# Where the weight differences of a Strassen-like down projection are made, and in which steps the work beside the second up phase is taken

## The chip, the cores and the metric

One core of a Trainium2 chip runs one program. The metric is the device time in microseconds (us) of one execution; the kernel before was run three times. PE is the matmul engine (PEld its weight loads), DVE the vector engine, ACT the scalar engine, POOL the GpSimd engine, SP the engine that issues most DMAs.

## What is computed

A residual block over 2048 positions of width 1024: a mixer (RG-LRU heads beside gMLP groups) and a gated feed-forward network, each between two RMS norms with scale, shift and gate from a conditioning vector.

```
h  = rmsnorm(x, g_mix_pre) * (1 + sc_m) + sh_m
z  = h @ w_in
y  = concat(rmsnorm(lru(z)), rmsnorm(gmlp(z))) @ w_out
x  = x + gt_m * rmsnorm(y, g_mix_post)
h  = rmsnorm(x, g_ffn_pre) * (1 + sc_f) + sh_f
up = causal_depthwise_conv(h @ w_up)        # 2 * 3072 columns, width 3
g_ff, v_ff = split(up)
y  = (gelu(g_ff) * v_ff) @ w_down           # 3072 -> 1024
x  = x + gt_f * rmsnorm(y, g_ffn_post)
```

Everything is float32. A product of two float32 operands is made of three matmuls: each operand is split into a high half (a cast on ACT) and a low half (source less high half, on DVE), and high*high, high*low and low*high are summed in PSUM.

## The kernel before

The positions are cut into 4 chunks of 512 for the mixer and 2 halves of 1024 for the feed-forward network. The program is one long list that is written out in Python; a planner then orders it by priority (the place in the list, less an offset where `high_priority` says so) with a model of the engines, lays the tiles into pools with a fixed number of slots, and adds the waits. Each engine, and each engine's DMA queue, runs its own list in order. Work that runs beside the main list is written as generators in a list `bg`; `tick()` takes one step of each, `drain()` takes all that are left on the spot.

**The mixer** (lines 830 to 854) takes chunk after chunk: `mixer_z(c)` makes z and its recurrences, `mixer_out(c - 1)` multiplies the chunk before by `w_out`. Beside them run the norms, the conditioning vectors (`ada_task`), and from c = 2 on `w_sums` (line 629). For each of 12 pairs of 128 rows of `w_down` it loads both rows whole (two DMAs of 512 KB on SP's queue), makes four differences of the two rows' halves (four POOL instructions of 128x512) and stores them (two DMAs of 512 KB on POOL's queue) in the DRAM tensor `wsd`. It waits for nothing, so that the planner may place it where POOL is idle, ahead of c = 2 too.

**The up phases** `up_phase(C, f0)` (line 1072), one for each half C of the positions, take 24 blocks f (from f = 2 on in the first) of the gated up projection as seven products instead of eight (`up_pair`, line 1041). Each block ends with a `tick()`. The weights' differences are made in the first and read back in the second. In the second, `first_finals` (line 1254) is started at f = 3: it makes the gate of the feed-forward network (`ada_task(5, 1)`, 21 steps) and then the last norm, gate and residual of the first half of the positions (`final`, line 1087, twice; 12 steps with those around it): 33 steps in all. `drain()` in line 1304 takes what is left after the phase.

**The down phases** `down_fast(C)` (line 1113) have seven products, in the order 11, s1/t1, s2/t2, s4/22, s3/t3, 12/21, 22/t4 (activation part / weight part). A product has 6 sets q, each of 24 matmuls (128x128 by 128x512). `operands` (line 1136) brings a set: an activation part (512 KB) and a weight part (512 KB) are loaded and split. For the four products whose weight part is a t, the weight part is read from `wsd`. Banks A and B of PSUM, four each, hold the sums. Beside the first down phase runs `h2_next`, which makes the activation parts of the second up phase.

Pools that matter: `tp` (36 slots, tag `t4`), `wp` (8, tag `w`: split halves), `rw` (4, tag `wraw`: raw weights), `lp` (3, tag `ld`), `rp` (6, tag `r`). A slot of `rw` is taken by `weight` (line 145) from the load until the low half is made.

Of the kernel before, what the change touches and what calls it, by code (L numbers as in the profile page):

```python
# [10 lines left out]
F32 = mybir.dt.float32  # L11
F32R = mybir.dt.float32r
AF = mybir.ActivationFunctionType
ALU = mybir.AluOpType

P = 128
# [7 lines left out]
NF = 24  # L24
# [16 lines left out]
def block_kernel(ctx: ExitStack, tc: tile.TileContext, xt, cols, rows, wada, wada_r, win_k, win_s, win_v, wgate, wsp, wout, wup, wdown, out):  # L41
# [3 lines left out]
    wp = ctx.enter_context(tc.tile_pool(name="wp", bufs=8))  # L45
    rw = ctx.enter_context(tc.tile_pool(name="rw", bufs=4))
# [7 lines left out]
    vec, act, pool, pe, sync = nc.vector, nc.scalar, nc.gpsimd, nc.tensor, nc.sync  # L54

    def t4(name):
        return tp.tile([P, 2, 512], F32, tag="t4", name=name)
# [25 lines left out]
    def tick():  # L83
        for g in list(bg):
            try:
                next(g)
            except StopIteration:
                bg.remove(g)

    def drain(*gens):  # L90
        for g in gens or list(bg):
            for _ in g:
                pass
            if g in bg:
                bg.remove(g)

    def start(*gens):
        bg.extend(gens)
        return gens
# [13 lines left out]
    def colr(name, j, n):  # L113
        o = _OFF[name] + j
        return prm[:, o:o + n]
# [17 lines left out]
    wsd = dram.tile([NF // 2, 2, P, ND, P], F32, name="wsd")  # L133


    def split(hi, lo, src, eng, leng=None):
        if eng == "act":
            act.copy(out=hi, in_=src)  # L138
        elif eng == "pool":
            pool.tensor_scalar(out=hi, in0=src, scalar1=1.0, scalar2=0.0, op0=ALU.mult, op1=ALU.add)  # L140
        else:
            vec.tensor_copy(out=hi, in_=src)
        (leng or vec).tensor_tensor(out=lo, in0=src, in1=hi.bitcast(F32), op=ALU.subtract)  # L143

    def weight(src, shape, name, eng="act", leng=None, mk=None, ahead=200, mkraw=None):
        with tc.high_priority(offset=ahead):
            raw = mkraw(f"{name}_r") if mkraw else rw.tile(shape, F32, tag="wraw", name=f"{name}_r")
            sync.dma_start(out=raw, in_=src)
            if mk is None:
                hi = wp.tile(shape, F32R, tag="w", name=f"{name}_h")  # L150
                lo = wp.tile(shape, F32R, tag="w", name=f"{name}_l")
            else:
                hi, lo = mk(shape, f"{name}_h"), mk(shape, f"{name}_l")
            split(hi, lo, raw, eng, leng)
        return hi, lo
# [79 lines left out]
    h = {}  # L235

    def x_rms(c, late=2):
        q = SumSq(f"n{c}")
        for j in range(4):
            q.add(load_x(xt, c, j, f"xq{c}"))  # L240
            yield
        yield
        hl = q.done()
        yield from wait(late)
        rx[c] = rms_bcast(hl, 1.0, f"n{c}", "rr", 4)
# [275 lines left out]
    def norm_scale(c, late=2):  # L521

        qs = []
        for tiles, name in zip(HU[c], (f"rl{c}", f"rg{c}")):
            qs.append(SumSq(name))
            for t in tiles:
                qs[-1].add(t)
            yield
        hls = [q.done() for q in qs]
        yield from wait(late)  # L530
        rs = [rms_bcast(hl, 2.0, f"r{n}{c}") for n, hl in zip("lg", hls)]
        yield
        for tiles, gname, r in zip(HU[c], ("g_lru_out", "g_gmlp_out"), rs):
            for j in range(2):
                for b in range(2):
                    t = tiles[j][:, b]
                    vec.scalar_tensor_tensor(out=t, in0=t, scalar=col(gname, 2 * j + b), in1=r, op0=ALU.mult, op1=ALU.mult)
                yield

    def norm_split(c):  # L540
        Y[c] = []
        mk = y4 if c == NC - 1 else h4
        for tiles, name in zip(HU[c], (f"rl{c}", f"rg{c}")):
            for j in range(2):
                yt = mk(f"{name}h{j}"), mk(f"{name}l{j}")
                split(yt[0], yt[1], tiles[j], "act")
                Y[c].append(yt)
                yield

    def mixer_norm(c, late=2):  # L550
        yield from norm_scale(c, late)
        yield from norm_split(c)
# [69 lines left out]
    def h_task(c, rms=True):  # L622
        if rms:
            yield from x_rms(c)
            yield
        h[c] = ([], [])
        yield from build_h(xt, c, h[c], sm, shm, f"x{c}")

    def w_sums():


        for p in range(NF // 2):
            e, o = [rw.tile([P, 8, P], F32, tag="wraw", name=f"ws{p}_{i}") for i in range(2)]
            sync.dma_start(out=e, in_=wdown[2 * p])
            sync.dma_start(out=o, in_=wdown[2 * p + 1])
            yield
            pool.tensor_tensor(out=e[:, :4], in0=e[:, 4:], in1=e[:, :4], op=ALU.subtract)
            pool.tensor_tensor(out=e[:, 4:], in0=o[:, 4:], in1=e[:, 4:], op=ALU.subtract)
            pool.tensor_tensor(out=o[:, 4:], in0=o[:, 4:], in1=e[:, :4], op=ALU.subtract)
            pool.tensor_tensor(out=o[:, :4], in0=o[:, :4], in1=o[:, 4:], op=ALU.subtract)  # L640
            pool.dma_start(out=wsd[p, 0], in_=e)
            pool.dma_start(out=wsd[p, 1], in_=o)
            yield


    wk, adat, acc0, adap = {}, {}, {}, {}

# [175 lines left out]
    for j in range(2):  # L823
        a = t4(f"xc0_{j}")
# [11 lines left out]
    for c in range(1, NC):  # L836
        nt = start(mixer_norm(0, 4) if c == 1 else norm_split(c - 1))
        xr = start(x_rms(c + 1, 8)) if c + 1 < NC else ()
        mixer_z(c)
        drain(*xr, *nt)  # L840
        if c == 1:
            m3, = start(ada_task(3, 1))
        if c == 2:
            m4, = start(ada_task(4, 1))
            wst = start(w_sums())
        if c + 1 < NC:
            ht = start(h_task(c + 1, False), norm_scale(c, 3))
            O, q = mixer_out(c - 1)
            drain(*ht)
            if c == 1:  # L850
                drain(m2)
                vec.tensor_tensor(out=gm, in0=modc[:, 16:24], in1=colr("g_mix_post", 0, 8), op=ALU.mult)
            start(mixer_post(c - 1, O, q))
# [218 lines left out]
    def up_phase(C, f0, on=lambda f: None):  # L1072
        before = None
        for f in range(f0, NF):
            on(f)
            g = up_pair(C, f)
            next(g)
            if before:
                drain(before)
            next(g)  # L1080
            before = g
            tick()
        drain(before)

    od = dram.tile([2, P, ND, 512], F32, name="od")
# [27 lines left out]
    def down_fast(C):  # L1113
# [13 lines left out]
        def w_src(k, q):  # L1127
            if k[0] == "t":
                i, h = {"t1": (0, 0), "t3": (0, 1), "t4": (1, 0), "t2": (1, 1)}[k]
                w = wsd[2 * q:2 * q + 2, i]  # L1130
            else:
                i, h = {"11": (0, 0), "21": (1, 0), "22": (1, 1)}[k]
                w = wdown[4 * q:4 * q + 4].rearrange("(a b) p d c -> a b p d c", b=2)[:, i]
            return w.rearrange("a p d c -> p a d c")[:, :, 4 * h:4 * h + 4]

        def operands(op, k, q):
            with tc.high_priority(offset=150):
                n = f"{op}_{q}"
                n = f"{C}{op}_{q}"
                first = op == "11" and q < 2  # L1140
                raw = t4(f"dgr{n}") if first or C == 0 else lp.tile([P, 2, 512], F32, tag="ld", name=f"dgr{n}")
                sync.dma_start(out=raw, in_=a_src(op, q))
                if C == 0:
                    g = [wp.tile([P, 2, 512], F32R, tag="w", name=f"dg{x}{n}") for x in "hl"]
                else:
                    g = h4(f"dgh{n}"), h4(f"dgl{n}")
                split(g[0], g[1], raw, "act")
                mkraw = (lambda m: tp.tile([P, 2, 4, P], F32, tag="t4", name=m)) if first else None
                w = weight(w_src(k, q), [P, 2, 4, P], f"dw{n}", ahead=0, mkraw=mkraw)
            return g, w  # L1150

        def mm(pt, g, w, a, d, first, stop):
# [91 lines left out]
        hl = rms_split(acc[1], "fr11")  # L1244
# [9 lines left out]
    def first_finals():  # L1254

        yield from ada_task(5, 1)
        vec.tensor_tensor(out=gf, in0=modc[:, 40:48], in1=colr("g_ffn_post", 0, 8), op=ALU.mult)
        for t in range(2):
            hl = rms_split(fsum[0][:, t], f"fr0{t}")
            yield  # L1260
            yield from final(0, t, [None] * 4, hl)
# [22 lines left out]
    O, q = mixer_out(NC - 2, True)  # L1284
# [15 lines left out]
    start(h2_next())  # L1300
    down_fast(0)
    drain()
    up_phase(1, 0, lambda f: start(first_finals()) if f == 3 else None)
    drain()
    down_fast(1)
    drain()
# [70 lines left out]
```

## Time and profile before

| | us |
|---|---|
| median of 3 runs | 2218.62 |
| lowest, highest | 2216.43, 2220.9 |
| the profiled execution | 2214.45 |
| its span, first to last instruction | 2212.4 |

| stage, read from the trace | from us | to us |
|---|---|---|
| mixer | 0 | 718 |
| first up phase | 718 | 1213 |
| first down phase | 1219 | 1450 |
| second up phase | 1450 | 1910 |
| second down phase and end | 1932 | 2212 |

The profile covers one execution. Its page gives the busy time of each engine; the views of the trace beside it give the busy time in chosen stretches, with the number of instructions, the granted clock of PE (1.00 is 2.4 GHz, 0.50 is 1.2 GHz) and the DMA engines' busy share; the groups of instructions by line; who waited for whom; the chain that ended last; and the instructions in order of time. Busy time of PE is modelled, so what a stretch has lost is better read from the number of its matmuls.

### The profile page before, as it was taken

Reading aid. Unit: us, or ns where it says so; the run is one execution under the profiler, and the core shown is the slowest. Engines: PE = TensorE matmul, PEld = TensorE weight load, DVE = VectorE, ACT = ScalarE, POOL = GpSimd, SP = SyncE. Lnnn points to the kernel's source line nnn. Section 1 sums busy time; section 2 is a strip of 40 time slices with the busy share of each in tenths; the row PEclk is TensorE's granted clock in tenths of the full one; section 3 lists DMA queues with packets and bytes.
Section 4 is the critical chain, followed back from the end, with each engine's and each line's share of the span. In section 5 each row is a group of like instructions: output and inputs, shape, how many; then the busy total and the mean of one; then the engine's idle time right before and its main releaser. Section 6 shows DMA issues by size and latency. Waiting matters only on the chain.

```text
span 2212.4 us, 24016 instructions
## 1 busy us (share of the span) xinstructions
PE 2013.4 (91%) x8744; PEld 1647.6 (74%) x8744; DVE 1565.4 (71%) x1703; ACT 950.1 (43%) x1224; POOL 525.1 (24%) x322
## 2 busy tenths in 40 slices
PE   5898948899999899999999999999999999669995
PEld 3686837777787788777877788888888888558884
DVE  7688698698385689998898766655555554754547
ACT  3472632433553555454554555443233333324432
POOL 4454264864320234434432000020000000000000
PEclk8998978998999999999999999999999999779998
DMA  8687578988766578979878656647777776686545
GB/s 316 200 307 279 181 256 309 336 313 309 271 253 242 183 272 330 338 282 360 325 288 316 240 202 217 228 157 256 272 254 264 256 269 241 218 301 212 179 164 152
DMA packets 192678, 572.46 MB, mean 259 GB/s; under 512 B 17456, under 2 KB 17584, under 8 KB 192560
## 3 DMA queue, kind: packets, MB, share of 16 engines
q1 hardware_dynamic: 180496, 527.93, 66.9%
q0 software_dynamic: 10912, 38.80, 4.7%
q10 hardware_dynamic: 1152, 4.19, 0.5%
q8 instruction: 69, 1.13, 0.2%
q14 instruction: 49, 0.40, 0.1%
HBM read 372.67 MB, written 199.23 MB: 259 GB/s over the span
## 4 chain that ended last, share of the span: by engine, by line
PE 59%; DVE 20%; DMA 7%; issue 6%; ACT 5%; POOL 2%; SPq 0%; DVEq 0%; ACTq 0%; POOLq 0%
PE dA L1155 10%; PE dB L1155 9%; PE upa L997 6%; PE upa L998 5%; PE upa L999 5%; PE upc L997 3%; PE upc L998 3%; PE upc L999 3%; DVE a L946 2%; PE upb L999 1%; PE upb L998 1%; DVE acc L665 1%; PE upb L997 1%; DVE x L256 1%; DMA xr<-in_xt_dram 1%
## 5 line engine op out<-in xcount | busy, mean ns | idle before, releaser
L946 DVE SCALAR_TENSOR_TENSOR a<-Rg,prm,a 128x1023 f32<-128x1023 f32 x92 | 127.1, 1382 | 99.3 <-ACT a L944 99.2
L1106 POOL DMA_DIRECT2D out_dram<-do x2 | 2.5, 1252 | 732.4 <-DVE do L1104 732.3
L977 POOL TENSOR_TENSOR wug<-wuv,wug 128x512 f32<-128x512 f32 x24 | 46.9, 1953 | 480.4 <-DVE w L143 480.4
L946 DVE SCALAR_TENSOR_TENSOR a<-Rv,prm,a 128x1023 f32<-128x1023 f32 x92 | 139.3, 1514 | 19.8 <-ACT a L944 19.4
L944 ACT ACTIVATE a<-Rv,prm 128x1024 f32<-128x1024 f32 x46 | 57.2, 1244 | 178.2 <-DVE Rv L1064 178.1
L1155 PE MATMUL dA<-dgh,dw_h 128*128 128x512 f32 x192 | 72.1, 411 | 37.6 <-ACT dw_h L138 19.5
L138 ACT CAST wt<-wug 128x512 fp32r<-128x512 f32 x72 | 44.7, 620 | 115.0 <-POOL wug L981 51.3
L143 DVE TENSOR_TENSOR wt<-wug,wt 128x512 fp32r<-128x512 f32 x72 | 67.9, 943 | 31.0 <-ACT wt L138 30.8
L1002 ACT ACTIVATE a<-a 128x1024 f32<-128x1024 f32 x48 | 50.9, 1060 | 75.9 <-DVE a L946 40.8
L1155 PEld LDWEIGHTS dA<-dgh,dw_h 128*128 128x128 f32 x192 | 38.0, 199 | 47.4 <-ACT dw_h L138 20.9
L143 DVE TENSOR_TENSOR dgl<-dgr,dgh 128x1024 fp32r<-128x1024 f32 x36 | 43.9, 1221 | 41.2 <-ACT dgh L138 41.2
L1155 PE MATMUL dA<-dgh,dw_l 128*128 128x512 f32 x192 | 70.7, 402 | 2.4 <-DVE dw_l L143 2.4
L1155 PE MATMUL dA<-dgl,dw_h 128*128 128x512 f32 x192 | 72.3, 405 | 0.0
L280 DVE SCALAR_TENSOR_TENSOR ada_m<-wada,cact,ada_m 128x1024 f32<-128x1024 f32 x28 | 50.1, 1789 | 27.6 <-DMA wada<-in_wada_r_dram 27.6
L138 ACT CAST dgh<-dgr 128x1024 fp32r<-128x1024 f32 x36 | 37.8, 1049 | 70.0 <-DMA dgr<-gd 30.0
L143 DVE TENSOR_TENSOR dw_l<-dw_r,dw_h 128x1024 fp32r<-128x1024 f32 x36 | 43.8, 1220 | 25.4 <-ACT dw_h L138 25.3
L1005 DVE TENSOR_TENSOR gg<-a,a 128x1024 f32<-128x1024 f32 x48 | 58.3, 1215 | 2.7 <-ACT a L1002 2.6
L944 ACT ACTIVATE a<-Rg,prm 128x1024 f32<-128x1024 f32 x46 | 57.1, 1242 | 1.3
L138 ACT CAST dw_h<-dw_r 128x1024 fp32r<-128x1024 f32 x36 | 37.5, 1047 | 45.1 <-DMA dw_r<-in_wdown_dram 16.2
L143 DVE TENSOR_TENSOR dw1s_l<-dw1s_r,dw1s_h 128x1024 fp32r<-128x1024 f32 x24 | 29.3, 1222 | 38.3 <-ACT dw1s_h L138 34.1
L222 POOL TENSOR_TENSOR rp_s<-rp_s,rp_s 128x1024 f32<-128x1024 f32 x12 | 30.0, 2499 | 91.0 <-ACT rp_s L218 90.9
L1068 ACT COPY Rg<-upa 128x512 f32<-128x512 f32 x46 | 26.8, 583 | 55.0 <-PE upa L999 55.0
(655 smaller groups left out, 6963.3 us busy)
## 6 DMA issues: line engine op xcount, KB each, us to landing
wkd<-wt SPq DMA_DIRECT2D x88, 512.0 KB, 3.8
wkd<-w SPq DMA_DIRECT2D x66, 512.0 KB, 4.6
w<-wkd SPq DMA_DIRECT2D x66, 512.0 KB, 4.1
gd<-gg SPq DMA_DIRECT2D x48, 512.0 KB, 4.4
gsd<-gg SPq DMA_DIRECT2D x48, 512.0 KB, 3.8
wrt<-wkd SPq DMA_DIRECT2D x44, 512.0 KB, 3.9
wt<-wkd SPq DMA_DIRECT2D x44, 512.0 KB, 4.4
dgr<-gd SPq DMA_DIRECT2D x36, 512.0 KB, 5.3
```

What stands on the lines that cost most here:

```text
L138: act.copy(out=hi, in_=src)
L143: (leng or vec).tensor_tensor(out=lo, in0=src, in1=hi.bitcast(F32), op=ALU.subtract)
L280: vec.scalar_tensor_tensor(out=flat, in0=w, scalar=cact[:, kt:kt + 1], in1=flat, op0=ALU.mult, op1=ALU.add)
L944: act.activation(out=a, in_=R, func=AF.Identity, scale=w[2], bias=col("ffn_conv_b", blk))
L946: vec.scalar_tensor_tensor(out=a[:, s:], in0=R[:, :FT - s], scalar=w[t], in1=a[:, s:], op0=ALU.mult, op1=ALU.add)
L977: pool.tensor_tensor(out=b11, in0=b12, in1=b11, op=ALU.subtract)
L997: pe.matmul(out=pt, lhsT=wh, rhs=mh, start=first and not more and k == 0, stop=False, skip_group_check=more)
L998: pe.matmul(out=pt, lhsT=wh, rhs=ml, start=False, stop=False, skip_group_check=more)
L999: pe.matmul(out=pt, lhsT=wl, rhs=mh, start=False, stop=last and k == 3, skip_group_check=more)
L1002: act.activation(out=g, in_=g, func=AF.Gelu_apprx_tanh)
L1005: vec.tensor_tensor(out=flat, in0=g, in1=v, op=ALU.mult)
L1155: pe.matmul(out=pt, lhsT=x[:, a, d], rhs=y[:, a], start=first and z == 0, stop=stop and z == 2, skip_group_check=True)
```

## The change

The generator `w_sums` is taken out of the mixer. In its place `operands` calls a new helper, `weight_sum`, for the weight parts t of the first down phase: it loads two weight parts as raw tiles from `rw` (a part of `w_down`, and another part or a t that was stored earlier), makes the difference on DVE, splits it, and stores it to `wsd` through ACT's DMA queue. The t4 product has no later reader, but its difference is stored in the same way for the second down phase; that phase reads `wsd` as before. In `up_phase` each block takes 1 + C ticks, so two in the second phase, and `first_finals` starts at f = 1 in place of f = 3. In `operands`, the split halves of the first two sets of product 11 come from `tp` in both phases: activation and weight halves in the first (they came from `wp`), weight halves in the second (its activation halves were there already).

```diff
@@ the mixer
-    def w_sums():
-        for p in range(NF // 2):
-            e, o = [rw.tile([P, 8, P], F32, tag="wraw", name=f"ws{p}_{i}") for i in range(2)]
-            sync.dma_start(out=e, in_=wdown[2 * p])
-            sync.dma_start(out=o, in_=wdown[2 * p + 1])
-            yield
-            pool.tensor_tensor(out=e[:, :4], in0=e[:, 4:], in1=e[:, :4], op=ALU.subtract)
-            pool.tensor_tensor(out=e[:, 4:], in0=o[:, 4:], in1=e[:, 4:], op=ALU.subtract)
-            pool.tensor_tensor(out=o[:, 4:], in0=o[:, 4:], in1=e[:, :4], op=ALU.subtract)
-            pool.tensor_tensor(out=o[:, :4], in0=o[:, :4], in1=o[:, 4:], op=ALU.subtract)
-            pool.dma_start(out=wsd[p, 0], in_=e)
-            pool.dma_start(out=wsd[p, 1], in_=o)
-            yield
...
             m4, = start(ada_task(4, 1))
-            wst = start(w_sums())
@@ up_phase
             next(g)
             before = g
-            tick()
+            for _ in range(1 + C):
+                tick()
@@ down_fast: w_src
-                i, h = {"11": (0, 0), "21": (1, 0), "22": (1, 1)}[k]
+                i, h = {"11": (0, 0), "12": (0, 1), "21": (1, 0), "22": (1, 1)}[k]
@@ down_fast
+        def weight_sum(k, q, name):
+
+            a, b = {"t1": ("12", "11"), "t2": ("22", "t1"), "t3": ("22", "12"), "t4": ("21", "t2")}[k]
+            raw, other = [rw.tile([P, 2, 4, P], F32, tag="wraw", name=f"{name}_{x}") for x in "ro"]
+            sync.dma_start(out=raw, in_=w_src(a, q))
+            sync.dma_start(out=other, in_=w_src(b, q))
+            vec.tensor_tensor(out=raw, in0=raw, in1=other, op=ALU.subtract)
+            hl = [wp.tile([P, 2, 4, P], F32R, tag="w", name=f"{name}_{x}") for x in "hl"]
+            split(hl[0], hl[1], raw, "act")
+            act.dma_start(out=w_src(k, q), in_=raw)
+            return hl
@@ operands
                 first = op == "11" and q < 2
+                mk = h_like if first else None
                 raw = t4(f"dgr{n}") if first or C == 0 else lp.tile([P, 2, 512], F32, tag="ld", name=f"dgr{n}")
                 sync.dma_start(out=raw, in_=a_src(op, q))
-                if C == 0:
+                if C == 0 and not first:
                     g = [wp.tile([P, 2, 512], F32R, tag="w", name=f"dg{x}{n}") for x in "hl"]
...
-                w = weight(w_src(k, q), [P, 2, 4, P], f"dw{n}", ahead=0, mkraw=mkraw)
+                if C == 0 and k[0] == "t":
+                    w = weight_sum(k, q, f"dw{n}")
+                else:
+                    w = weight(w_src(k, q), [P, 2, 4, P], f"dw{n}", ahead=0, mkraw=mkraw, mk=mk)
@@ the end of block_kernel
-    up_phase(1, 0, lambda f: start(first_finals()) if f == 3 else None)
+    up_phase(1, 0, lambda f: start(first_finals()) if f == 1 else None)
```

## Rows read from the trace of the kernel before

**Rows 1.** The page's first part: busy us, share of the span, instructions.

```profile
PE 2013.4 (91%) x8744; PEld 1647.6 (74%) x8744; DVE 1565.4 (71%) x1703; ACT 950.1 (43%) x1224; POOL 525.1 (24%) x322
```

**Rows 2.** Busy time by stretch: length, engines (instructions), PE clock, DMA share, GB/s.

```profile
300.00:340.00 40.00, 2.70 (x8) 1.21 (x7) 37.44 (x23) 9.27 (x11) 25.34 (x19) 0.57 0.67 240
340.00:520.00 180.00, 165.85 (x708) 135.23 (x709) 150.05 (x132) 68.69 (x81) 116.20 (x79) 0.92 0.89 328
520.00:800.00 280.00, 263.92 (x1156) 216.10 (x1155) 184.33 (x195) 129.22 (x164) 80.83 (x33) 0.98 0.68 249
850.00:1200.00 350.00, 337.13 (x1456) 274.12 (x1456) 317.55 (x325) 177.99 (x289) 144.04 (x74) 0.99 0.87 322
1200.00:1260.00 60.00, 51.67 (x216) 41.45 (x215) 42.95 (x44) 32.08 (x41) 0.00 (x0) 0.94 0.66 233
1270.00:1450.00 180.00, 180.00 (x795) 148.84 (x794) 113.34 (x111) 90.35 (x105) 1.51 (x2) 1.00 0.60 208
1500.00:1880.00 380.00, 380.00 (x1678) 314.70 (x1678) 206.89 (x287) 116.31 (x140) 0.00 (x0) 1.00 0.75 260
1900.00:1990.00 90.00, 50.39 (x191) 38.76 (x190) 62.72 (x70) 27.75 (x27) 0.00 (x0) 0.73 0.80 286
```

**Rows 3.** POOL groups, 280 to 520: busy us, mean ns, idle before.

```profile
L639 POOL TENSOR_TENSOR ws<-ws,ws 128x512 f32<-128x512 f32 x12 | 18.2, 1513 | 0.7
...
L638 POOL TENSOR_TENSOR ws<-ws,ws 128x512 f32<-128x512 f32 x12 | 16.3, 1359 | 27.1 <-DMA ws<-in_wdown_dram 27.1
```

**Rows 4.** DVE in order of time, 285 to 345: start, us, what.

```profile
300.11 11.59 DVE L256 SCALAR_TENSOR_TENSOR x<-x,sm,n_r 128x512 f32<-128x512 f32 x2 [1.72 <-DMA x<-in_xt_dram]
...
327.14 11.14 DVE L537 SCALAR_TENSOR_TENSOR r<-r,prm,rl_r 128x512 f32<-128x512 f32 x4
```

**Rows 5.** POOL in order of time, 285 to 345.

```profile
301.59 1.27 POOL L638 TENSOR_TENSOR ws<-ws,ws 128x512 f32<-128x512 f32 x1
```

**Rows 6.** Groups of all engines, 1860 to 1990.

```profile
L1104 DVE SCALAR_TENSOR_TENSOR fo<-fo,gf,fr_r 128x512 f32<-128x512 f32 x16 | 10.8, 743 | 0.0
...
L1109 DVE TENSOR_TENSOR fo<-fo,fx 128x1024 f32<-128x1024 f32 x8 | 9.8, 1221 | 8.7 <-DMA fx<-x2d 8.6
...
L206 DVE RECIPROCAL fr_r<-fr_r 128x512 f32<-128x512 f32 x2 | 6.7, 3344 | 0.0
```

**Rows 7.** Waits, 280 to 345 us: us in total, times, longest.

```profile
PE rg_m L202 <- DVE rg_hl L142: 19.6, 1, 19.6
PE rl_m L202 <- DVE rl_hl L142: 15.2, 1, 15.2
```

**Rows 8.** Waits of PE, 340 to 560.

```profile
PE g L179 <- ACT vv L437: 6.4, 1, 6.4
```

**Rows 9.** The chain that ended last, 340 to 525: start, us, what.

```profile
409.22 10.80 DMA xr<-in_xt_dram
```

**Rows 10.** DMA issues, 1220 to 1450: KB each, median us to landing.

```profile
dw0s_r<-wsd SPq DMA_DIRECT2D x18, 512.0 KB, 4.0
```

**Rows 11.** Groups of DVE, 1220 to 1450.

```profile
L143 DVE TENSOR_TENSOR dw0s_l<-dw0s_r,dw0s_h 128x1024 fp32r<-128x1024 f32 x24 | 29.3, 1219 | 0.7 <-ACT dw0s_h L138 0.7
```

**Rows 12.** DMAs that ACT issues in the mixer: issue ns, smallest, median, largest.

```profile
L885 ACTq DMA_DIRECT2D hs<-xf x8: 326/326/486, 615.9 to 715.2; - x8
```

**Rows 13.** Waits of SP's queue, 1220 to 1450.

```profile
SPq L148 <- DVE dw0s_l L143: 83.4, 24, 6.2
```

**Rows 14.** Groups of ACT, 1220 to 1450.

```profile
L138 ACT CAST dw0s_h<-dw0s_r 128x1024 fp32r<-128x1024 f32 x24 | 25.1, 1047 | 0.0
```

**Rows 15.** DMA issues, 1000 to 1100.

```profile
wkd<-w SPq DMA_DIRECT2D x15, 512.0 KB, 7.2
wug<-in_wup_dram SPq DMA_DIRECT2D x5, 512.0 KB, 6.2
```

**Rows 16.** Waits, 1900 to 1990.

```profile
PE dA L1155 <- ACT dgh L138: 18.1, 1, 18.1
```

**Rows 17.** Waits of PE, 1200 to 1460.

```profile
PE dA L1155 <- ACT dw_h L138: 7.5, 2, 6.7
```

## The prediction

> **What bounds the kernel now.** Start with the page's first part [rows 1]: PE is busy for 91% of the span and DVE for 71%. That is an average over unlike stages, so next cut the span into stretches [rows 2] and read the matmul counts. Where PE never stops it runs 1678 matmuls in 380 us, 4.416 per us or 0.2265 us each; a set of 24 takes 5.43 us. What a stretch lacks of that pace is its loss, half clock included:
>
> - 300 to 340: 8 of 177 matmuls, 38 us lost; granted clock 0.57, so the 1.2 GHz level for most of it.
> - 340 to 520: 708 of 795, 20 us lost. 520 to 800: 1156 of 1236, 18 us.
> - 850 to 1200 (first up phase, DVE 91% busy): 1456 of 1546, 20 us or 5.8%.
> - 1200 to 1260 (up to down, first half): 216 of 265, 11 us.
> - 1270 to 1450 (first down phase): 795 of 795, nothing; DVE 63% busy. 1500 to 1880 (second up phase): nothing; DVE 54%.
> - 1900 to 1990 (up to down, second half): 191 of 397, 47 us at clock 0.73.
>
> So PE is the bound, and what can be won lies in three places: the mixer's holes and the two passages from up to down. What can be lost lies in the first down phase, which has no hole today. The waits then say what stands behind each hole.
>
> **Part 1: `w_sums` leaves the mixer.** It removes 48 POOL instructions, 16 to 18 us for each of four groups of 12 (the dearest and the cheapest in [rows 3]), 69 us in all, and 48 DMAs of 512 KB (25 MB) on SP's and POOL's queues from a stretch whose DMA engines are 0.89 busy [rows 2]. POOL is not on PE's path. DVE is, and it pays for POOL: two DVE instructions at 300.11 took 11.59 us and four at 327.14 took 11.14 us [rows 4], while POOL ran tensor instructions, a ws among them at 301.59 [rows 5]. The `fo` group of the same kind and size takes 0.743 us each with POOL idle [rows 6], so the six should take 4.5 us, and 18 us are delay. PE stood waiting for just these results, 15.2 and 19.6 us [rows 7]. Of POOL's tensor work in the two places about half is ws, the rest (squares, splits of `w_out`) stays. So I give back 10 us of the 38. From below: 5, if the remaining POOL work fills the same place; from above: 18. In 340 to 520, PE's longest wait is 6.4 us for a gelu [rows 8]; the chain ahead of it holds a load of x that took 10.8 us to land [rows 9], against 4.0 us for a load of that size in a quiet stretch [rows 10]. With 25 MB fewer I give back half of the 20 us: 10 (3 to 17). In 520 to 800, where no ws runs, 1 (-3 to 5). Term: -21, from -5 to -40.
>
> The Trainium skill has a rule for the DVE rows. By "SBUF — State Buffer", section "Who interferes with whom", a DVE instruction with two SBUF inputs and a GpSimd instruction that reads SBUF exclude each other for a whole instruction. The trace agrees in kind (5.8 us in place of 0.74 on average for the first pair). Taken at its word, all POOL time of ws goes back to DVE, which is the first rival.
>
> **Part 2: the differences move into the first down phase.** Four products of 6 sets get one: 24 times. Per set it adds on DVE one subtraction of 128x1024, as long as the low half it feeds, 1.22 us [rows 11]: 29 us. On ACT it adds a DMA issue, 0.33 us [rows 12]: 8 us, behind a cast that waited for the same subtraction anyway, so nothing new queues behind a wait. On SP's queue it adds a load per set, with the activation loads, the loads of `h2_next` and the stores of the phase behind it. The phase gains 24 loads and 24 stores, 25 MB; spread over its 232 us that is 108 GB/s on top of 208, near the 322 that the first up phase moves at share 0.87 [rows 2].
>
> DVE: in a t set its load rises by 1.22/5.43 = 22 points, to 85%. The nearest row is the first up phase, 91% busy with PE losing 5.8%; over 24 sets (130 us) that is 7.6 us at most, and 0 at least, if the new subtraction falls into the idle time while DVE waits for a cast.
>
> Slots of `rw`: before, a set took one of four slots, and SP waited for them 24 times (83 us) without PE noticing [rows 2, 13]. Now a set takes two. The second operand's is held for load and subtraction, the first's for load, subtraction, cast (1.05 us [rows 14]), issue and landing of the store. With quiet landings of 4.0 us [rows 10]: 4.0 + 1.2 + 1.05 + 0.33 + 4.0 = 10.6, and 5.2; 15.8 slot-us over four slots is 4.0 us per set, under PE's 5.43: nothing lost. With landings as in the busy first up phase, 6.2 for loads and 7.2 for stores [rows 15]: 16.0 and 7.4, 5.85 us per set, 0.42 too slow, 24 times: 10 us. If the first operands only ever follow each other through two slots, 16.0/2 = 8.0 us per set, 62 us lost. I take the middle row, 10, since the phase's new DMA load is that of the first up phase, and 2 for DVE, whose waits mostly fall into the same time. Term: +12, from 0 to +62.
>
> On the store's queue the Trainium skill speaks against the change. "DMA: Bandwidth & Descriptors", section "Issuing engines are not separate DMA queues", says that DMAs of all queues run on the same 16 engines, so that another queue saves only issue time. By it the stores through ACT slow the loads as if SP had issued them, and the sum is the 10 us above; were ACT's queue a road of its own, landings would stay quiet and it would be 0.
>
> **Part 3: two ticks per block, from f = 1.** Before, 21 blocks took 21 of the 33 steps, and the other 12, both finals, were drained between the phases. There they cost DVE 10.8 + 9.8 + 6.7 us [rows 6], and SP eight loads, followed by eight loads of x and eight stores; PE waited 18.1 us for the first cast of the down phase [rows 16]. After, 23 blocks offer 46 ticks for 33 steps: all finals are done by about block 18. What is late next is the down phase's own start, as at the first passage, which has no finals and loses 11 us. So the 47 us become 11: -36 (from -44, if nothing is left, to -25, if SP's order keeps the loads late). In the second up phase the moved 31 us of DVE lie beside PE with DVE 54% busy, and 24 DMAs (12.6 MB) beside a DMA share of 0.75 [rows 2]. PE can notice it through the 3.3 us reciprocals, which delay the release of PSUM banks, and through `tp`: of 36 slots 28 hold activation halves and one the sum of squares, and a block needs four of the seven left at its peak; the finals take two or three. I charge 2 us (0 to 25). If that cover goes, it is the second rival.
>
> **Part 4: halves of the first two sets in `tp`.** The first matmul of the first down phase waited 6.7 us for a cast [rows 17]. The cast needs a slot, its load and the gelu ahead of it in ACT's list, and only the slot is changed; slots of `tp` come free as the last block's products end. I give 2 us at each passage, -4 in all (from -12 to +6).
>
> **Sum.** -21 + 12 - 36 + 2 - 4 = -47 us on the profiled execution's 2214.5: 2167.5. The median of the runs lies 4.2 us above that execution, so I expect a median of 2172.
>
> **The rivals.**
> 1. *POOL's lock was dearer than I took it.* All 69 us of ws come back to DVE; PE's loss from 300 to 520 is 58 us, and five sixths of it go. For it: DVE is 94% busy from 300 to 340. Against it: half of POOL's work stays in those places, and part of the holes are latencies. Part 1 is then -50: 2143.
> 2. *The finals are not hidden, only moved.* Each of eight steps stalls PE for 2 us and each reciprocal for 3.3: 23 us in the second up phase, in place of 2. For it: the tightness of `tp` and the order of DVE's list. Against it: the first ada steps ran there without a loss. 2193.
> 3. *The raw slots set the pace of the first down phase*, as the 8.0 us case above: +62, and holes of 2.6 us in each set may let the clock fall as at 0.73 in the second passage; at 0.85 over 130 us that is 23 more. 2218.6 - 59 + 85 = 2245. It decides from 5.43 + 59/24 = 7.9 us per set. For it: SP's 24 waits show that slots already gate loads; against it: landings must stay busy and the slots must be dealt out badly.
> 4. *The change does not do what it says at the second passage*: the first operands of the down phase wait for something other than the finals, and 20 us stay beside the first passage's 11. 2192.
>
> **How the numbers follow.** Chances: the forecast 0.62 (own range 2155 to 2188), rival 1 0.14, rivals 2 and 4 together 0.17, rival 3 0.05, and 0.02 that the parts cancel. The range 2142 to 2200 leaves out rival 3, the cancelling case and the far ends of the others. A measurement of this kernel tells about 0.2% (4.4 us) from no change: faster 0.93, same 0.02, slower 0.05.
>
> **What would show it.** Part 1: 300 to 340 holds well over 8 matmuls, and the DVE instructions of lines 256 and 537 come near 0.75 us. Part 2: matmuls per set in the first down phase stay near 5.4 us apart in the products 11, 22 and 21, and near 5.9 in the t products, with SP waiting for a store to land. Part 3: no `fo` after the last up matmul, and the second passage loses about as much as the first. Part 4: the first cast of each down phase comes earlier after the last up matmul. The forecast is wrong if the first down phase grows by over 30 us, or if the second up phase, now without a hole, gets some.

## The result and the profile after

The changed kernel takes 2166.4 us (median of 4 runs, 2157.6 to 2167.4) against 2218.6 before: a ratio of 0.9756, 95% interval 0.9728 to 0.9783. The profiled execution took 2167.4 us, 47.0 less than that of before. So the time came out as forecast; the places did not. Cut both traces where the same matmul starts, and the difference goes to its stages:

| from, to (start of the named matmul) | before, us | after, us | difference | forecast |
|---|---|---|---|---|
| start, first up matmul | 726.1 | 682.6 | -43.5 | -21 |
| to the first matmul of the first down phase | 493.5 | 494.9 | +1.4 | -2 |
| to the first of the second up phase | 235.6 | 260.9 | +25.3 | +12 |
| to the last s3 product of the second up phase | 450.8 | 452.8 | +2.0 | +2 |
| to the first s1 matmul of the second down phase | 85.9 | 52.7 | -33.2 | -38 |
| to the end of the span | 220.5 | 221.7 | +1.2 | 0 |

The mixer gave twice what was forecast, the first down phase took twice, and the errors of the stages sum to almost nothing. One limit of such a table: seven other kernels below have the mixer of the changed kernel, and their first up matmul comes at 676.3 to 681.1 us, so that a few us of difference in that stage say nothing.

First the rows behind the table, from the view by operation of single tiles (duration ns, then first and last start in us): the first down phase starts at 1177.5, the second up phase at 1438.4, the s1 product of the second down phase at 1943.9.

```profile
L1155 PE MATMUL dA<-dgh,dw_h x192: 387/390/797, 1177.5 to 2139.5; 128*128 128x512 f32 x192
...
L980 PE MATMUL upc<-hs_10h,wt x48: 388/389/390, 1438.4 to 1876.2; 128*128 128x512 f32 x48
...
L1155 PE MATMUL dB<-dgh1s,dw1s_h x96: 388/390/390, 1943.9 to 2041.1; 128*128 128x512 f32 x96
```

Stretches of [rows 2] in the changed kernel; those of the later stages are moved by about as much as their stage starts earlier (columns as there):

```profile
300.00:340.00 40.00, 27.47 (x108) 21.30 (x107) 34.68 (x35) 18.61 (x22) 15.81 (x9) 0.83 0.80 294
340.00:520.00 180.00, 178.09 (x798) 147.48 (x797) 152.16 (x161) 73.76 (x86) 63.19 (x23) 0.99 0.71 258
...
1228.00:1408.00 180.00, 165.80 (x690) 133.52 (x688) 120.77 (x117) 83.03 (x97) 0.00 (x0) 0.95 0.84 290
1483.00:1863.00 380.00, 380.00 (x1681) 314.87 (x1681) 234.07 (x319) 121.43 (x145) 0.00 (x0) 1.00 0.81 291
1883.00:1973.00 90.00, 77.37 (x325) 62.82 (x324) 47.15 (x48) 35.36 (x37) 0.00 (x0) 0.94 0.62 205
```

Read the matmul counts. From 300 to 340 there are 108 in place of 8, from 340 to 520 there are 798, the full pace of 795: of the 58 us lost there, 16 are left. The first passage (1158 to 1218) has 213, nearly as before. The first down phase, which had 795 of 795, now has 690, with the clock at 0.95: that is the new loss. The second up phase still has none, with the finals in it. The second passage has 325 in place of 191; 397 would be full.

The new loss has two parts. Cut at its own ends, the phase holds the same matmuls in both kernels, before and after:

```profile
1219.00:1455.00 236.00, 234.15 (x1020) 192.58 (x1021) 156.39 (x153) 125.11 (x149) 5.81 (x4) 0.99 0.61 211
```

```profile
1177.00:1438.00 261.00, 243.85 (x1019) 196.56 (x1020) 183.69 (x177) 125.85 (x149) 5.52 (x4) 0.96 0.85 296
```

PE stands idle for 17.2 us in place of 1.9, and the same matmuls keep it busy 9.7 us longer, at a mean granted clock of 0.96 in place of 0.99. So of the 25 us about 15 are waits and about 10 are matmuls at the lower of the two clocks. The loss is uneven: of the four products with a t part, s1/t1 takes 37.0 us in place of 32.5, s2/t2 43.8 in place of 32.6 (clock 0.88), s3/t3 38.1 in place of 32.8 and 22/t4 35.1 in place of 32.6.

What PE waits for in the first down phase (us in total, times, longest), and what ACT waits for most:

```profile
PE dA L1155 <- ACT dw_h L138: 9.3, 4, 6.7
PE dA L1155 <- ACT dw0s_h L138: 8.3, 5, 4.1
...
ACT dw0s_h L138 <- DVE dw0s_r L1126: 22.3, 11, 4.1
```

6.7 us of the first row are the phase's first matmul, as in [rows 17]. `dw0s_h` is the high half of a weight part; ACT makes it by a cast, and the cast waits for the new subtraction (line 1126). Why the subtraction is late stands in SP's queue (start, us, what), in the t2 product:

```profile
1261.02 0.36 SPq L1125 DMA_DIRECT2D dw0s_o<-wsd  x1
...
1270.77 0.36 SPq L1125 DMA_DIRECT2D dw0s_o<-wsd  x1
...
1280.62 0.36 SPq L1125 DMA_DIRECT2D dw0s_o<-wsd  x1
```

and in DVE's list:

```profile
1269.52 1.22 DVE L1126 TENSOR_TENSOR dw0s_r<-dw0s_r,dw0s_o 128x1024 f32<-128x1024 f32 x1
...
1279.37 1.22 DVE L1126 TENSOR_TENSOR dw0s_r<-dw0s_r,dw0s_o 128x1024 f32<-128x1024 f32 x1 [2.14 <-DMA dw0s_o<-wsd]
```

The load of the second operand at 1270.77 follows the subtraction that began at 1269.52 and gave the slot back; it lands after 8.5 us, the next subtraction starts at 1279.37, and the next load follows it at 1280.62. Here the second operand's loads come 9.8 and 9.9 us apart, where PE uses up a set in 5.43. That is the loop over `rw` slots, in the order of SP's list. In the whole phase second operands' loads waited twelve times for a subtraction as the last thing (15.0 us), and loads of weight parts ten times for the store of a sum to land (29.2 us).

### The profile page after: what moved, and what is told of

Its sections match the earlier page's. It is cut to its first block, busy times and chain, and to the rows that moved or that the text cites. A ratio compares the mean times of both kernels' runs of the same rounds, so it can differ in the third digit from the quotient of the medians.

```text
span 2165.6 us, 23968 instructions
## 1 busy us (share of the span) xinstructions
PE 2014.3 (93%) x8744; PEld 1649.3 (76%) x8744; DVE 1553.9 (72%) x1727; ACT 953.6 (44%) x1226; POOL 440.0 (20%) x250
## 4 chain that ended last, share of the span: by engine, by line
PE 62%; DVE 17%; DMA 10%; issue 5%; ACT 4%; POOL 1%; SPq 0%; DVEq 0%; ACTq 0%; POOLq 0%
PE dA L1155 9%; PE upa L980 6%; PE upa L982 6%; PE upa L981 6%; PE dB L1155 5%; PE upc L980 3%; PE upc L981 3%; PE upc L982 3%; DVE a L929 2%; PE upb L982 1%; PE upb L981 1%; PE upb L980 1%; DMA dw0s_o<-in_wdown_dram 1%; PE lg L179 1%; PE lg L180 1%
## 5 line engine op out<-in xcount | busy, mean ns | idle before, releaser
L929 DVE SCALAR_TENSOR_TENSOR a<-Rv,prm,a 128x1023 f32<-128x1023 f32 x92 | 139.2, 1513 | 20.7 <-ACT a L927 20.3
L280 DVE SCALAR_TENSOR_TENSOR ada_m<-wada,cact,ada_m 128x1024 f32<-128x1024 f32 x28 | 45.1, 1612 | 29.2 <-DMA wada<-in_wada_r_dram 29.2
L143 DVE TENSOR_TENSOR dw_l<-dw_r,dw_h 128x1024 fp32r<-128x1024 f32 x36 | 43.9, 1220 | 29.0 <-ACT dw_h L138 28.8
```

Of the source, the lines that this page charges most:

```text
L280: vec.scalar_tensor_tensor(out=flat, in0=w, scalar=cact[:, kt:kt + 1], in1=flat, op0=ALU.mult, op1=ALU.add)
L929: vec.scalar_tensor_tensor(out=a[:, s:], in0=R[:, :FT - s], scalar=w[t], in1=a[:, s:], op0=ALU.mult, op1=ALU.add)
```

## The experiments

The kernel before ran beside each group: 2215.4 us (median of 13 runs) beside the first four, 2215.1 (9) beside the next four, 2216.9 (7) beside the last three. Theories: **A**, in the mixer POOL's instructions hold up DVE and through it PE; **B**, the mixer's 25 MB of DMAs do. **S**, the slots of the raw weights set the first down phase's pace; **V**, DVE's new work does; **D**, the new traffic does.

### The parts alone

**e_steps**, only the steps of the second up phase:

```diff
@@ up_phase
-            tick()
+            for _ in range(1 + C):
+                tick()
...
-    up_phase(1, 0, lambda f: start(first_finals()) if f == 3 else None)
+    up_phase(1, 0, lambda f: start(first_finals()) if f == 1 else None)
```

> The kernel before with two ticks per block of the second up phase and the finals from f = 1, and nothing else of the change. Theory (finals drained between the phases were the second passage's stall): the last matmul of the second up phase to the first s1 matmul of the second down phase shrinks by 33 us, the second up phase grows by 2 us, all else stays: 2218.6 - 31 = 2188 us. Rival (the passage waits for the down phase's own operands): at most 15 us are won, 2204 or more. The traces of the changed kernel leave 33 us for this place, but there the other parts were changed too.

2177.8 us, ratio 0.9828 (0.9811 to 0.9846): 37.6 us faster. From the last s3 product of the second up phase to the s1 product it takes 46.4 us in place of 85.9, the second up phase 452.8 in place of 450.8, and no other stage moves by over 1.6 us. The finals drained between the phases were 39.5 us of the passage; the rival is out. The stretch of [rows 2] in this kernel now holds 353 of 397 matmuls:

```profile
1900.00:1990.00 90.00, 82.41 (x353) 67.39 (x352) 50.26 (x51) 41.50 (x45) 0.00 (x0) 0.96 0.64 222
```

**e_sums**, only the weight sums moved: the changed kernel with one tick per block, `f == 3`, and the first halves' old tiles (the diff of the change without those lines).

> The kernel before with the weight sums moved out of the mixer and into the first down phase, without the other two parts. Theory (the parts add up): first up matmul 43 us earlier, first down phase 25 us longer, the rest unchanged: 2218.6 - 18 = 2200 us. If the tiles of the first halves were needed for either number: the first down phase longer by 35 us or more and 2210 or above.

2194.6 us, ratio 0.9902 (0.9882 to 0.9923): 20.7 us faster. First up matmul at 679.2 (47 us earlier), first down phase 263.0 us (27 longer), second passage 85.9 as before. So the gain in the mixer and the loss in the first down phase belong together and need neither other part.

**e_halves**, only the other tiles:

```diff
                 first = op == "11" and q < 2
+                mk = h_like if first else None
...
-                if C == 0:
+                if C == 0 and not first:
...
-                w = weight(w_src(k, q), [P, 2, 4, P], f"dw{n}", ahead=0, mkraw=mkraw)
+                w = weight(w_src(k, q), [P, 2, 4, P], f"dw{n}", ahead=0, mkraw=mkraw, mk=mk)
```

> The kernel before with the halves of the first two sets in the other pool, and nothing else. As the prediction had it: 2 us at each passage, 2214.6. Rival (the slot never was what the first cast waited for; the load and the gelu ahead of it were): within 2 us of 2218.6, and the first matmul of each down phase waits as long as before (6.7 us in the first).

2216.4 us, ratio 0.9999 (0.9988 to 1.0009). The rival holds: the phase's first matmul waits for the same cast as long as it did [rows 17]:

```profile
PE dA L1156 <- ACT dw_h L138: 8.3, 2, 6.7
```

In the kernel before, that cast starts at 1218.53, directly behind the last gelu of the up phase in ACT's list (1217.57, 1.06 us long), and the gelu had waited for DVE. So at this passage the gelu came last, not the slot.

### What the mixer gave back

**e_nosub**, the kernel before without the subtractions:

```diff
             yield
-            pool.tensor_tensor(out=e[:, :4], in0=e[:, 4:], in1=e[:, :4], op=ALU.subtract)
-            pool.tensor_tensor(out=e[:, 4:], in0=o[:, 4:], in1=e[:, 4:], op=ALU.subtract)
-            pool.tensor_tensor(out=o[:, 4:], in0=o[:, 4:], in1=e[:, :4], op=ALU.subtract)
-            pool.tensor_tensor(out=o[:, :4], in0=o[:, :4], in1=o[:, 4:], op=ALU.subtract)
             pool.dma_start(out=wsd[p, 0], in_=e)
```

> The kernel before with the 48 POOL subtractions of the mixer left out, its 48 DMAs kept (so the t weight parts are plain rows). Theory A (POOL's instructions hold up DVE, and DVE holds up PE): nearly the whole of the mixer's 43 us is won, 35 to 43: 2176 to 2184. Theory B (the 25 MB of DMAs delay the loads that DVE and ACT wait for): less than 10 us, 2209 or more. In between, both share it.

2180.4 us, ratio 0.9837 (0.9819 to 0.9855): 35.0 us faster; first up matmul at 689.1, 37 of the changed kernel's 43.5 us. From 280 to 520 the DMA engines are busier than before, and PE runs more all the same:

```profile
280.00:520.00 240.00, 219.35 (x964) 179.68 (x963) 191.10 (x205) 91.91 (x107) 99.24 (x62) 0.96 0.95 355
```

964 matmuls in place of 808 in the kernel before, at a DMA share of 0.95 in place of 0.84; the loads of `w_down` themselves land after 10.1 us. Theory A. One DVE group shows it, in the kernel before and here (busy us, mean ns):

```profile
L612 DVE SCALAR_TENSOR_TENSOR oo<-oo,gm,rp_r 128x512 f32<-128x512 f32 x8 | 15.4, 1996 | 0.0
```

```profile
L612 DVE SCALAR_TENSOR_TENSOR oo<-oo,gm,rp_r 128x512 f32<-128x512 f32 x16 | 15.1, 1012 | 0.0
```

The same instruction takes 2.00 us with the subtractions on POOL and 1.01 without (0.74 with POOL idle, [rows 6]), so that DVE gets 16 done in the window where it got 8. How much it comes to is seen in all of DVE's work up to the first up matmul, the same 591 instructions in both kernels (columns as in [rows 2], DVE's the third):

```profile
0.00:726.10 726.10, 611.30 (x2651) 497.23 (x2651) 551.51 (x591) 323.91 (x383) 328.17 (x217) 0.92 0.76 275
```

```profile
0.00:689.10 689.10, 608.62 (x2650) 497.51 (x2650) 505.82 (x591) 323.19 (x382) 255.06 (x169) 0.95 0.79 290
```

They take 45.7 us less. DVE's waits for results of POOL, 4.2 us from 280 us on, are the same in both. One thing is mixed in: without the subtractions the planner also orders DVE's list otherwise. The cast that PE waited 19.6 us for [rows 7] started at 339.40 before, behind the four instructions of line 537 [rows 4]; here it starts at 320.92, ahead of them.

**e_nodma**, the converse: one pair of tiles, loaded once, all 48 subtractions on it, no store.

```diff
         for p in range(NF // 2):
-            e, o = [rw.tile([P, 8, P], F32, tag="wraw", name=f"ws{p}_{i}") for i in range(2)]
-            sync.dma_start(out=e, in_=wdown[2 * p])
-            sync.dma_start(out=o, in_=wdown[2 * p + 1])
+            if p == 0:
+                e, o = [rw.tile([P, 8, P], F32, tag="wraw", name=f"ws{p}_{i}") for i in range(2)]
+                sync.dma_start(out=e, in_=wdown[2 * p])
+                sync.dma_start(out=o, in_=wdown[2 * p + 1])
...
-            pool.dma_start(out=wsd[p, 0], in_=e)
-            pool.dma_start(out=wsd[p, 1], in_=o)
...
-                w = wsd[2 * q:2 * q + 2, i]
+                w = wdown[4 * q:4 * q + 4].rearrange("(a b) p d c -> a b p d c", b=2)[:, i]
```

> The kernel before with the mixer's 48 POOL subtractions kept, but all on one pair of tiles that is loaded once and never stored; 46 of the 48 DMAs are gone and the down phases read plain rows for the t parts. Theory A (POOL against DVE): at most 10 us are won, 2209 or more, perhaps less since the subtractions no longer wait for loads and come in a bunch. Theory B (DMA traffic): 33 us or more are won, 2186 or less.

2208.3 us, ratio 0.9964 (0.9950 to 0.9978): 6.9 us faster; first up matmul at 717.6, 8.5 us of the 43.5. DMA share 0.66 from 280 to 520, and only 838 matmuls. DVE's 591 instructions take 549.8 us, nearly as before. This kernel's list has the cast of [rows 7] ahead of line 537 too (329.21 against 336.17), so that the new order there, without the relief from POOL, is worth little. So about 37 us are POOL's instructions and about 8 the DMAs, each good to a few us, and they nearly add (45.5 against 43.5).

### What the first down phase took

**e_nows**, the changed kernel with the t parts read as rows of `w_down`, no sums:

```diff
-                w = wsd[2 * q:2 * q + 2, i]
+                w = wdown[4 * q:4 * q + 4].rearrange("(a b) p d c -> a b p d c", b=2)[:, i]
...
-                if C == 0 and k[0] == "t":
-                    w = weight_sum(k, q, f"dw{n}")
-                else:
+                if True:
                     w = weight(w_src(k, q), [P, 2, 4, P], f"dw{n}", ahead=0, mkraw=mkraw, mk=mk)
```

> The changed kernel with no weight sums at all: the t parts are read as plain rows of w_down, one load each, as the kernel before read its stored sums. Theory (the whole cost of the first down phase, 25 us, is the sums made there): 2166.4 - 25 = 2141 us, first down phase as long as in the kernel before (227 to 230 us from its first matmul to the first of the second up phase's t1). If part of the cost came from the other two parts of the change: above 2150.

2138.5 us, ratio 0.9655 (0.9637 to 0.9673); the first down phase takes 236.1 us, as in the kernel before (235.6). All 25 us are the sums.

**e_rp**, the second operand in another pool:

```diff
-            raw, other = [rw.tile([P, 2, 4, P], F32, tag="wraw", name=f"{name}_{x}") for x in "ro"]
+            raw = rw.tile([P, 2, 4, P], F32, tag="wraw", name=f"{name}_r")
+            other = [rp.tile([P, 4, P], F32, tag="r", name=f"{name}_o{x}") for x in range(2)]
             sync.dma_start(out=raw, in_=w_src(a, q))
-            sync.dma_start(out=other, in_=w_src(b, q))
-            vec.tensor_tensor(out=raw, in0=raw, in1=other, op=ALU.subtract)
+            for x in range(2):
+                sync.dma_start(out=other[x], in_=w_src(b, q)[:, x])
+            for x in range(2):
+                vec.tensor_tensor(out=raw[:, x], in0=raw[:, x], in1=other[x], op=ALU.subtract)
```

> The changed kernel with the second operand of each difference in two half tiles of the pool r (6 slots, little used in this phase) in place of the raw weights' pool; two half loads of 256 KB, two half subtractions on DVE (0.69 us each, 0.15 us more per set). Theory S (the raw weights' four slots set the pace): a set takes one slot again, and 15 to 25 us come back: 2141 to 2151. Theories V (DVE's added work) and D (25 MB more DMA traffic): nothing comes back, 2163 to 2172.

2148.4 us, ratio 0.9699 (0.9680 to 0.9717). The first down phase takes 247.7 us in place of 260.9: 13 of the 25 us come back, with the same traffic and slightly more work on DVE. That is a little less than the 15 to 25 that were named; the run gained 18, but 5 of them in the mixer, where the kernels do not differ. Theory S for that half, though the loads were halved in size along with it, which no run separates. The whole phase has as many matmuls (1019) as that of the changed kernel (its row stands in the section before) in 13 us less, at a higher DMA rate; 7 of the 13 us are idle time of PE and 6 slower matmuls:

```profile
1171.00:1419.00 248.00, 237.86 (x1019) 194.32 (x1020) 185.24 (x201) 125.94 (x149) 5.59 (x4) 0.98 0.86 307
```

**e_nostore**, the changed kernel without the stores:

```diff
-                w = wsd[2 * q:2 * q + 2, i]
+                w = wdown[4 * q:4 * q + 4].rearrange("(a b) p d c -> a b p d c", b=2)[:, i]
...
             split(hl[0], hl[1], raw, "act")
-            act.dma_start(out=w_src(k, q), in_=raw)
```

> The changed kernel without the 24 stores of the sums; where an earlier sum is read, plain rows are read instead, so that the loads, the subtractions and the splits are all there. Theory S (slots): the raw tile is free about 6 us earlier in each set; of 16 + 7 slot-us 17 + 0 remain, under PE's pace: 12 to 25 us come back, 2141 to 2154. Theory D (traffic; 12.6 of 25 MB gone): 5 to 12 us. Theory V (DVE): nothing, 2163 to 2168.

2145.5 us, ratio 0.9685 (0.9666 to 0.9704); first down phase 242.1 us: 19 of the 25 us come back. DVE's work is all there, so V alone is out. It does not part S from D, since half of the added traffic went too; e_rp does.

**e_rp_nosub**, e_rp without its subtraction (the two lines of `vec.tensor_tensor` taken out):

> The changed kernel with the second operand in the pool r and the subtraction left out (the t parts are plain rows; all loads and stores stay). With the slots relieved, the first down phase is still 12 us longer than in the kernel before (247.7 against 235.6 us). Theory V (DVE's 29 us of subtractions): 8 to 12 us come back, 2136 to 2140. Theory D (25 MB more traffic): under 4 us, 2145 to 2149.

2152.0 us, ratio 0.9710 (0.9694 to 0.9726): not faster than e_rp. The first down phase shrinks from 247.7 to 242.2 us, 5.5 of the remaining 12, but the kernel reaches it 7.4 us later, since one wait for the cast of a first set there grew to 14.2 us in the newly ordered lists. As V foresaw the phase gets shorter, by less than it said; the time as a whole speaks for neither. On balance about half of the remaining 12 us is DVE. Where the rest lies can be seen: in e_rp the 12 us were lost in the products s2/t2, s3/t3 and 22/t4 (5.2, 1.3 and 4.4 us) and in the first one; here PE never stops from s2/t2 on, beside the same traffic:

```profile
1255.10:1419.00 163.90, 163.90 (x724) 135.51 (x723) 105.89 (x104) 83.85 (x99) 3.87 (x3) 1.00 0.86 304
```

All that is lost, 6.6 us, is lost in s1/t1, where e_rp lost nothing. So the traffic alone did not hold up the last three t products; what did it in s1/t1 stays open.

### Whether the other tiles cost something

**e_no4**, the changed kernel with the first halves' old tiles (the diff of e_halves, taken back):

> The changed kernel without the new tiles for the first halves (the other two parts stay). Alone, that part moved nothing (2216 against 2215). But from the last matmul of the second up phase to the first s1 matmul of the second down phase the changed kernel takes 52.7 us, and the kernel with the new steps alone 46.4. Theory (freed wp slots let loads for later sets go ahead of the second set's weight load on SP's queue, and the part costs 6 us there): 46 us again, 2157 to 2161 where the changed kernel has 2163 to 2166. Rival (the difference comes from the sums or from a shifted order): 52 us stay, no change.

2159.4 us (2154.4 to 2163.3), ratio 0.9749 (0.9726 to 0.9772), which is not to be told from the changed kernel's 0.9756. In the place that the theory names it is: 45.9 us from the last s3 product to the s1 product in place of 52.7. The waits of PE there, in the changed kernel and in this one:

```profile
PE dA L1155 <- ACT dw_h L138: 11.8, 2, 8.2
```

```profile
PE dA L1154 <- ACT dw_h L138: 6.8, 1, 6.8
```

The second wait is gone. It is the same in the other kernels: with parts 3 and 4 together this passage takes 51.1 to 53.2 us (five kernels, one of them without any sums), with part 3 and the old tiles 45.9 to 46.4 (three). In the changed kernel SP issues the second set's weight load only at 1909.38, behind loads of later sets' t parts that began at 1883.88 and behind a store at 1909.00; without the new tiles it goes out before them, and the first of those t parts is loaded at 1905.34. The rest of this run's gain is not part 4's: its mixer, untouched by the part, ended 5 us earlier.

**e_rp_no4**, e_rp with the first halves' old tiles:

> The changed kernel with the second operand in the pool r and without the new tiles for the first halves. If the two add: 2148.4 - 6 = 2142 us, the fastest version here that computes the whole block. If the 6 us are a shifted order: 2146 to 2150.

2144.9 us (2139.7 to 2145.9), ratio 0.9673 (0.9654 to 0.9692), the fastest version here that computes the whole block, though its interval overlaps with that of e_rp. The second passage takes 46.3 us again and the first down phase 246.2.

## Why the prediction was right, and where it was not

**Part 1, the mixer: right mechanism, half the size.** -21 was forecast, -43.5 measured, beyond the lower bound of -40. The step that failed is the halving, in both places. From 300 to 340 I saw 18 us of delay in two DVE rows [rows 4] and gave back 10, because half of POOL's work there is not `ws` and would keep DVE waiting. Of the 18 us 14.5 went: line 256's two instructions take 5.46 us in place of 11.59, line 537's four 2.73 in place of 11.14.

```profile
306.20 5.46 DVE L256 SCALAR_TENSOR_TENSOR x<-x,sm,n_r 128x512 f32<-128x512 f32 x2 [4.21 <-DMA x<-in_xt_dram]
...
329.20 2.73 DVE L537 SCALAR_TENSOR_TENSOR r<-r,prm,rl_r 128x512 f32<-128x512 f32 x4
```

The pair of line 256 does not come near the 0.75 us each that the prediction named as a sign; POOL's remaining tensor work still lies beside it, from 302.8 to 310.4. From 340 to 520 I put what could be won down to the traffic. But e_nosub, with a DMA share of 0.97 there, runs 779 matmuls in place of 708, so 16 of the 20 us come back with all the traffic kept, and in the whole mixer the traffic is worth 8 (e_nodma). The two rows that I read were a sample: over all of DVE's list the delay is 46 us (e_nosub), not 18. The first rival, -50, was nearer than the forecast, although it too was not exact: of POOL's 69 us, 46 came back to DVE, and the first up matmul came 37 earlier. Part of that is the new order of DVE's list, which the prediction did not foresee and no run separates in full.

The Trainium skill's rule on this ("SBUF — State Buffer", section "Who interferes with whom": a DVE instruction with two SBUF inputs and a GpSimd instruction that reads SBUF shut each other out), taken at its word as in that rival, would have given the better number for this part. The runs agree in kind: 2.00 us against 1.01 for the group of line 612.

**Part 2, the first down phase: right mechanism, half the size.** +12 was forecast, +25.3 measured. The landings were priced well: loads of raw parts took 6.1 us (6.2 assumed), the stores 6.2 (7.2 assumed). Two steps failed. The first is that the forecast priced waits alone. PE's idle time grew by 15.3 us, not far from the 12; the other 9.7 are matmuls at the lower clock, which the sum put at nothing and only the third rival charged. The second is the even pace of 5.85 us a set, 23 slot-us over four slots, which supposes that any free slot serves any operand at once. In SP's list the loads have a fixed order; loads waited for the subtraction before them and for a store, and each holds up those behind it. Measured were 25.3 us over 24 sets, 6.5 us a set on average, clock included, but 7.3 in s2/t2 and 5.9 in 22/t4; the first lies near the 8.0 of the third rival. Why s2/t2 has it worst stays open. e_rp and e_nostore bear the slots out. DVE's share was put at 2; e_rp_nosub makes it about 5.

On the store's queue the trace agrees with the Trainium skill ("DMA: Bandwidth & Descriptors", section "Issuing engines are not separate DMA queues"): the loads of raw parts that SP issues land after 6.1 us beside the stores that ACT issues, and after 4.5 us in e_nostore, which has as many loads and no stores.

**Part 3, the finals: right.** -36 and +2 were forecast. Alone the part gives -39.5 in the passage and +2.0 in the second up phase; in the changed kernel -33.2 and +2.0, since part 4 costs 6 to 7 us there. The second rival is out: the second up phase runs 1681 matmuls in 380 us, as many as before. So is the fourth: the part alone leaves 353 of 397 matmuls in the passage, a loss of 10 us, as much as the 11 that the first passage loses.

**Part 4, the halves: wrong sign.** -4 was forecast, "only the slot is changed" among three things the cast waits for; the slot was not the one that came last; at the first passage the gelu was. Alone it moves nothing, beside part 3 it costs 6 to 7 us in the second passage, which lies just beyond the upper end of +6.

**The sum** was right by luck, because the terms' errors cancel: -22.5 in the mixer, +13.3 in the first down phase, +4.8 in the second passage, +3.4 from the first up phase to the first down phase and +1.2 at the end.

## What to carry to other kernels

Work on POOL that "fills idle time" can be paid for by DVE. Where DVE is the engine that PE waits for, look at all of DVE's instructions beside that work and not only at those ahead of the longest wait: here the two rows of the prediction showed 18 us of delay, the whole list had 46, and 37 of them were the kernel's. When an operand is doubled, count slots in the order of the queue that loads them, not as a sum of slot time over slots: a load in order behind one that waits for a slot waits too; putting the second operand in an idle pool gave half of the loss back. Do not price holes as waits alone: here 15 us of waits came with 10 us of matmuls at a lower clock. Background work that is left over at a phase's end stands between the phases: 12 steps cost 39.5 us there and 2.0 us beside the phase; count its steps against the phase's ticks.

## What the runs showed of the hardware

One and the same load, 512 KB of a raw weight part in the first down phase, landed later the more moved beside it: a median of 4.1 us at 221 GB/s (e_nows), 4.5 at 267 (e_nostore), 6.1 at 296 (the changed kernel). The rate does not fix it alone: 5.3 us at 306 GB/s in e_rp, and the activation loads of the same size beside it in the changed kernel took 7.9. In the mixer the loads of `w_down` took 10.1 us at 355 GB/s (e_nosub); from 280 to 520 PE lost 22 us there, against 57 before and 14.5 in the changed kernel.

DVE instructions of one shape took far longer beside tensor work on POOL: 11.59 us for two of 128x512 [rows 4], 1.97 us for the same two without the subtractions (e_nosub), and 0.74 us each where POOL was idle [rows 6].
